# Sample attention's tables made in the projections and kept in memory, x2's first part normalised beside sample attention, and gating sums taken three chunks at a time

## The chip, the cores and the metric

The kernel runs on one core of one Trainium2 chip, as one program. The metric is the device time of one execution in microseconds (us). A core has TensorE (PE; its weight loads are listed as PEld), VectorE (DVE), ScalarE (ACT), GpSimd (POOL), SyncE (SP, which only issues transfers) and 16 DMA engines. Each engine takes its instructions in the order in which they stand.

## The reference, cut to what matters

One layer of a hybrid decoder for a prompt (1024 rows) and a sample group (8 sequences of 8 new rows, 2048 past rows in a paged cache), 1088 rows in all, width 1024, everything in float32:

```python
x = x + 0.5 * swiglu(rmsnorm(x)) @ wd            # FFN1, width 2816
u = rmsnorm(x) @ w_in                            # q, k/v of three branches, gates, z, xBC, dt
y = rmsnorm_groups(ssd(silu(conv(xBC))) * silu(z)) * ssm_norm      # Mamba-2, 8 heads, chunks of 128
o = g0 * compressed(q) + g1 * selected(q) + g2 * window(q)         # attention, with ALiBi slopes
x = x + concat(o, y) @ w_out
x = x + 0.5 * swiglu(rmsnorm(x)) @ wd2           # FFN2
out = rmsnorm(x)
```

For the sample rows attention needs constant tables: ALiBi biases by position (for compressed, selected, window and new rows), masks, a triangle for ranking the blocks, and one-hot matrices that spread gates and sum groups of rows. They depend on no input but their shape.

## The kernel before, in words

Activations lie transposed: features on the 128 partitions, rows along the free dimension, 1088 of them in two halves `b` of 544, each half in two parts (`SUBS`: 256 and 288 columns). x lies in `xT`, eight tiles of 128 features. Part z=0 is the first 256 columns of each half, z=1 the other 288. Products in float32 are made of three products of a high part (`whi`, `hh`, `oh`) and a low part (`wlo`, `hl`, `ol`), in `mm3` (L237); ScalarE casts the high part and VectorE or POOL subtracts for the low one (L229, L258). The FFNs go through 2x2 blocks with seven products (`B1`..`B7`, `dq`).

A scheduler places the instructions: the code's order is the starting point, and the order on each engine comes from a planner with its own costs. The kernel's stages, in time:

1. FFN1, then its down projection (`D1.products`, L590): products into `dq` on TensorE, eight banks; VectorE adds each to xT (L618).
2. The norm of x: for each feature tile ScalarE squares and POOL or VectorE adds into `rms` (`row_sq`, L768), the scaled x is split into `hh` and `hl` (`row_split`, L778). `rms_row` (L803) sums over the partitions with five small products against `ones` (bank `nps`), takes the root and the reciprocal, and spreads the factor over the partitions by products with `ident` (`nR`). The half b=1 comes first, then b=0.
3. Projections: eight xBC groups (L238; `xbc_chunk` evacuates a bank into `xr`, which takes the factor `rms`), convolution, then z, then the Mamba scan (`scan`, L1069). `mamba_setup` makes `BD`, six 32x512 blocks of decay sums in bfloat16 (`blocks_of`, L1051), which the first products `ar` (L1105) of chunks 0 to 7 read.
4. Keys and values (`proj`, `keys`, `cmp_products`), and between them `gate` (L1196) for each of nine chunks: z from memory into `za`, times y, square on ScalarE, one addition (L1203), two sums over the partitions by products against `ones` (bank `yn`, L1206), a copy into `yr`. After chunks 6 and 8 the root and reciprocal, and products `yR` that spread the factor.
5. q, then the prompt's attention in eight tiles of 128 queries (`KN["qt"]`), with the sample's compressed rows between. The last tile ends it. VectorE takes the maximum of each score bank, ScalarE the exponential (L1660), POOL or VectorE scales, TensorE transposes (`pT`) and multiplies by the values (`o`).
6. Sample attention (`sample_attention`, L1716): first its tables (`bsel`, `bwin`, `bnew`, `bcmp`, `tri`, `G`, `E`, `hsel`, `idx4`, `oneh`), then, for four pairs of sequences, rows gathered by POOL's indirect transfers (`schk`), and scores. Between them stand the output projection's products (`wout`): y for z=0, attention's rows for z=0, y for z=1. With each z=0 tile of x2 that is done, ScalarE squares and VectorE adds into `acc20` (`x2_sq`, L2075).
7. The rest of the output projection (attention's rows for z=1), beside which z=0's norm is finished (`x2_rms(0)`), its eight rows of h are made in `hp` (`h_row`, L2149) and split into B1..B7 (`b0`, L2160), and z=1's squares are added into `acc` (L2084). `x2_rms(1)` follows, and FFN2 begins with `g` (L398).
8. FFN2 and the last norm.

Pools hand memory on: a tile of a new pool waits for the last use of what lay there before.

Of the kernel before, what the change touches and what calls it, by code (L numbers as in the profile page):

```python
# [17 lines left out]
P = 128  # L18
# [62 lines left out]
def hybrid_step(ctx: ExitStack, tc: tile.TileContext, *aps):  # L81
# [16 lines left out]
    zD = DR.tile([4, P, T], F32, name="zD")  # L98

# [703 lines left out]
    def rms_row(v, n):  # L803

        q = side("nps")
        parts = blocks(n)
        for i, m in parts:
            nc.tensor.matmul(q[:m, i:i + 1], v[:, P * i:P * i + m], ones[:, :1], start=True, stop=True,
                             skip_group_check=True)
# [27 lines left out]
    WA = Ahead(Ws.enter_context(pool("w", bufs=8, side="right")))  # L837
# [25 lines left out]
    with pool("cv", bufs=2) as K:  # L863
# [39 lines left out]
        stT = K.tile([P, 8, 24], F32, name="stT", bufs=1)  # L903
        for group in [(0, 1)] + [(i,) for i in range(2, 8)]:
# [9 lines left out]
            for i in group:  # L914
                xbc_end(i, *ws[i][1:])
        for z in range(2):
# [33 lines left out]
    def mamba_setup(K, K2, Q, acs_bank):  # L950
# [100 lines left out]
        def blocks_of(z):  # L1051
# [12 lines left out]
        for z in range(2):  # L1064
            blocks_of(z)
# [130 lines left out]
    def gate(K, yr, c):  # L1196
# [6 lines left out]
        nc.vector.tensor_tensor(za[:, ::2, :L], za[:, ::2, :L], za[:, 1::2, :L], op=OP.add)  # L1203
        q = side("yn")
        for g in range(2):
            nc.tensor.matmul(q[:L, g:g + 1], za[:, 2 * g, :L], ones[:, :1], start=True, stop=True,  # L1206
                             skip_group_check=True)
        nc.vector.tensor_copy(yr[:L, c], q[:L, :2])
        if c in (6, 8):
            v = yr[:, :7] if c == 6 else yr[:, 7:]  # L1210
            nc.vector.tensor_scalar(v, v, 1.0 / 256, EPS, op0=OP.mult, op1=OP.add)
            nc.scalar.activation(v, v, AF.Sqrt)
            nc.vector.reciprocal(v, v)
            t0, n = SUBS[c // 8]
            for t0 in (t0, HALF + t0):
# [58 lines left out]
    with pool("kvtmp", bufs=2) as K:  # L1274
# [118 lines left out]
        for c in range(2):  # L1393
            gate(K, yr, c)
# [5 lines left out]
        for c in range(2, 4):  # L1400
            gate(K, yr, c)
# [6 lines left out]
        for c in range(4, 7):  # L1408
            gate(K, yr, c)
        cmp_finish(1, ab)  # L1410
        v2 = proj(2, 1)
        keys(2, k2)
        natural(2, (k2, v2))
        for c in range(7, 9):
            gate(K, yr, c)
    Ds = ExitStack()
# [913 lines left out]
```

## Time and profile before

| | |
|---|---|
| median of 3 runs | 2544.39 us (2540.56 to 2546.0) |
| the profiled execution's own time | 2548.51 us |
| its span in the profile | 2546.8 us, mean granted clock 0.971 |
| TensorE busy | 2439.3 us (96%) |
| VectorE busy | 1759.6 us (69%) |
| ScalarE busy | 1116.8 us (44%) |
| POOL busy | 430.4 us (17%) |
| moved by DMA | 371.90 MB, 146 GB/s |

Times in the rows are counted from the start of the span. A row of a timeline is a group of equal neighbours: start, time from the first's start to the last's end, engine, line, operation, result from operands, count; in brackets the idle time before it and what released it. Neighbours on one engine overlap by some hundredths of a microsecond. [...]

### The profile page before, as it was taken

Reading aid. Unit: us, or ns where it says so; the run is one execution under the profiler, and the core shown is the slowest. Engines: PE = TensorE matmul, PEld = TensorE weight load, DVE = VectorE, ACT = ScalarE, POOL = GpSimd, SP = SyncE. Lnnn points to the kernel's source line nnn. Section 1 sums busy time; section 2 is a strip of 40 time slices with the busy share of each in tenths; the row PEclk is TensorE's granted clock in tenths of the full one; section 3 lists DMA queues with packets and bytes.
Section 4 is the critical chain, followed back from the end, with each engine's and each line's share of the span. In section 5 each row is a group of like instructions: output and inputs, shape, how many; then the busy total and the mean of one; then the engine's idle time right before and its main releaser. Section 6 shows DMA issues by size and latency. Waiting matters only on the chain.

```text
span 2546.8 us, 48004 instructions
## 1 busy us (share of the span) xinstructions
PE 2439.3 (96%) x18979; PEld 2241.6 (88%) x18979; DVE 1759.6 (69%) x3676; ACT 1116.8 (44%) x2461; POOL 430.4 (17%) x530
## 2 busy tenths in 40 slices
PE   6999999999999989899999998998799999999998
PEld 6999999999999978898677766566799999999998
DVE  6767677677777655666566677666877776768776
ACT  7544444441242253225566675443544444443113
POOL 0000000011133343434333342221100000001110
PEclk9999999999999999999999999899899999999999
DMA  4334343597652323323010110666233444459754
GB/s 164 123 125 160 126 159 133 176 354 283 223 185 80 104 72 113 94 79 116 34 67 34 42 59 1 222 201 210 79 112 131 156 146 153 149 190 372 254 207 150
DMA packets 226269, 371.90 MB, mean 146 GB/s; under 512 B 18173, under 2 KB 143785, under 8 KB 224892
## 3 DMA queue, kind: packets, MB, share of 16 engines
q1 hardware_dynamic: 207112, 311.92, 35.8%
q0 software_dynamic: 7600, 38.59, 4.3%
q10 hardware_dynamic: 11332, 18.33, 1.9%
q8 instruction: 149, 2.44, 0.4%
q14 instruction: 76, 0.62, 0.1%
HBM read 250.84 MB, written 122.07 MB: 146 GB/s over the span
## 4 chain that ended last, share of the span: by engine, by line
PE 83%; DVE 8%; ACT 3%; DMA 3%; issue 1%; POOL 0%; ACTq 0%; DVEq 0%; SPq 0%; POOLq 0%
PE gY L353 6%; PE gY L354 6%; PE gY L352 6%; PE dq L609 5%; PE dq L610 5%; PE dq L611 5%; PE gX L353 4%; PE gX L354 4%; PE gX L352 4%; PE o L1691 3%; PE pT L1682 3%; PE s L1644 1%; PE cA L1569 1%; PE xbc L238 1%; PE cA L1571 1%
## 5 line engine op out<-in xcount | busy, mean ns | idle before, releaser
L610 PE MATMUL dq<-db,da 128*128 128x256 f32 (+1 forms) x1232 | 352.8, 287 | 0.3 <-DVE da L258 0.3
L611 PE MATMUL dq<-db,da 128*128 128x256 f32 (+1 forms) x1232 | 352.4, 287 | 0.0
L609 PE MATMUL dq<-db,da 128*128 128x256 f32 (+1 forms) x1232 | 349.0, 288 | 2.9 <-DVE xT L255 1.5
L618 DVE TENSOR_TENSOR xT<-xT,dq 128x256 f32<-128x256 f32 (+1 forms) x456 | 186.6, 434 | 82.7 <-PE dq L611 81.0
L609 PEld LDWEIGHTS dq<-db,da 128*128 128x128 f32 x1232 | 229.8, 188 | 4.2 <-DVE xT L255 1.7
L258 POOL TENSOR_TENSOR ds<-dw 128x512 f32<-128x512 f32 x22 | 28.6, 1299 | 1208.2 <-DMA dw<-in_ffn_wd_dram 988.4
L611 PEld LDWEIGHTS dq<-db,da 128*128 128x128 f32 x1232 | 232.3, 189 | 0.0
L610 PEld LDWEIGHTS dq<-db,da 128*128 128x128 f32 x1232 | 231.2, 188 | 0.6 <-DVE da L258 0.5
L255 ACT CAST whi<-ws 128x512 fp32r<-128x512 f32 x156 | 96.4, 622 | 210.5 <-PE gY L354 144.7
L258 DVE TENSOR_TENSOR wlo<-raw,whi 128x512 fp32r<-128x512 f32 x180 | 123.0, 688 | 79.2 <-ACT whi L255 78.9
L255 ACT CAST da<-ds 128x512 fp32r<-128x512 f32 x88 | 52.8, 626 | 236.9 <-PE dq L611 92.5
L255 ACT CAST whi<-raw 128x512 fp32r<-128x512 f32 x184 | 113.9, 625 | 65.9 <-PE gY L354 20.0
L1660 ACT ACTIVATE pb<-s,mx 128x256 f32<-128x256 f32 (+3 forms) x192 | 105.1, 552 | 74.3 <-DVE mx L1658 38.8
L258 DVE TENSOR_TENSOR wlo<-ws,whi 128x512 fp32r<-128x512 f32 x156 | 106.8, 688 | 42.2 <-ACT whi L255 41.7
L1682 PEld LDWEIGHTS pT<-ident,pb 128*128 128x128 f32 x528 | 60.8, 147 | 49.7 <-issue 40.9
L1657 DVE TENSOR_REDUCE mx<-s 128x1 f32<-128x384 f32 (+2 forms) x128 | 66.6, 536 | 40.8 <-PE s L1649 27.5
L1682 PE MATMUL pT<-ident,pb 128*128 128x128 f32 x528 | 90.8, 290 | 3.5 <-ACT pt L255 1.5
L352 PE MATMUL gY<-B3h,whi 128*128 128x256 f32 (+1 forms) x320 | 91.5, 287 | 1.4 <-ACT whi L255 1.4
L353 PE MATMUL gX<-B6h,wlo 128*128 128x256 f32 (+1 forms) x320 | 91.8, 287 | 0.5 <-DVE wlo L258 0.5
L352 PE MATMUL gX<-B6h,whi 128*128 128x256 f32 (+1 forms) x320 | 91.4, 286 | 0.9 <-ACT Cc L359 0.9
L353 PE MATMUL gY<-B3h,wlo 128*128 128x256 f32 (+1 forms) x320 | 91.7, 287 | 0.2 <-DVE wlo L258 0.2
L353 PE MATMUL gY<-B2h,wlo 128*128 128x256 f32 (+1 forms) x320 | 91.8, 287 | 0.0
(714 smaller groups left out, 8603.5 us busy)
## 6 DMA issues: line engine op xcount, KB each, us to landing
db<-GD SPq DMA_DIRECT2D x42, 1632.0 KB
GD<-Cc SPq DMA_DIRECT2D x154, 272.0 KB
GD<-his SPq DMA_DIRECT2D x84, 272.0 KB
raw<-in_ffn_wg_dram SPq DMA_DIRECT2D x22, 1024.0 KB
raw<-in_ffn_wu_dram SPq DMA_DIRECT2D x22, 1024.0 KB
dw<-in_ffn_wd_dram SPq DMA_DIRECT2D x44, 512.0 KB
GD<-hp SPq DMA_DIRECT2D x70, 272.0 KB
db<-GD SPq DMA_DIRECT2D x14, 1088.0 KB
```

The costliest lines, as they stand in the source:

```text
L255: return nc.scalar.copy(out, src) if eng == "a" else ENGINES[eng].tensor_copy(out, src)
L258: ENGINES[eng].tensor_tensor(out, x, y, op=op)
L352: nc.tensor.matmul(q, ah[:, k], b_, start=first, stop=False, skip_group_check=True)
L353: nc.tensor.matmul(q, al[:, k], b_, start=False, stop=False, skip_group_check=True)
L354: nc.tensor.matmul(q, ah[:, k], c_, start=False, stop=(k == 3), skip_group_check=True)
L609: nc.tensor.matmul(q, x, bh[:, u, o], start=first, stop=False, skip_group_check=True)
L610: nc.tensor.matmul(q, y, bh[:, u, o], start=False, stop=False, skip_group_check=True)
L611: nc.tensor.matmul(q, x, bl[:, u, o], start=False, stop=(u == np_ - 1), skip_group_check=True)
L618: nc.vector.tensor_tensor(x, x, q, op=OP.subtract if i == 4 else OP.add)
L1660: nc.scalar.activation(pb[:, st:st + pn], s, AF.Exp, bias=mx[:, 0:1], accum_out=part[:, hh_, i:i + 1])
L1682: nc.tensor.transpose(tq_[:kn, P * hh_:P * hh_ + P], src, ident)
L1691: mm = nc.tensor.matmul(O[64 * u:64 * u + 64], v_, p_, start=(ui < 2), skip_group_check=True, stop=(ui - len(held) + 1 + u >= len(units) - 2))
```

## The change

Four parts.

- **Tables.** `sample_constants` holds what stood at the head of `sample_attention`. It is called within the xBC groups, after group 3; all but `idx4` and `oneh` go into slices of one tile `big` (128 x 4552 float32), which is written to memory (`saD`). In sample attention `big` is read back. The pool of weight tiles `w` has 7 buffers in place of 8.
- **Decay blocks.** The six multiplications of `BD` are POOL's, and the `bd_b` tile has three buffers.
- **Gating.** `gate` leaves the added squares of a chunk in `hs`; `gate_sums` makes the products for three chunks in one bank, with one copy; `gate_norm` takes the root and spreads the factors once, at the end.
- **The second norm.** z=0's norm stands right after z=0's last tile of x2, and its rows of h overwrite x2's z=0 tile (which is first stored to `xD`). For z=1 TensorE sums the squares: five products per tile add up in one bank (`sums`), and VectorE's additions into `acc` are gone. The pools `x20`, `ha` and `wa` are opened in another order, and `acc20` lies in `ha`.

```diff
@@ projections
-    WA = Ahead(Ws.enter_context(pool("w", bufs=8, side="right")))
+    WA = Ahead(Ws.enter_context(pool("w", bufs=7, side="right")))
...
+        def sample_constants(SC, Q):
+            big = Q.tile([P, 4552], F32, name="big")
...
+            nc.vector.tensor_tensor(bsel, bc[:, None, :].to_broadcast([P, 16, P]),
+                                    bs[:, :, None].to_broadcast([P, 16, P]), op=OP.add)
...
+            nc.sync.dma_start(saD, big)
+            return idx4, oneh
...
+            if group[0] == 3:
+                with pool("sac0") as Q:
+                    sa_const = sample_constants(M, Q)
@@ mamba_setup
-                b = Q.tile([96, P], BF16, name="bd_b", bufs=1)
+                b = Q.tile([96, P], BF16, name="bd_b", bufs=3)
...
-                nc.vector.tensor_tensor(D[d], b[d, None, :].to_broadcast([32, 4, P]),
+                nc.gpsimd.tensor_tensor(D[d], b[d, None, :].to_broadcast([32, 4, P]),
                                         hm[d, :, None].to_broadcast([32, 4, P]), op=OP.mult)
@@ gating
-    def gate(K, yr, c):
+    def gate(K, hs, c):
...
-        nc.vector.tensor_tensor(za[:, ::2, :L], za[:, ::2, :L], za[:, 1::2, :L], op=OP.add)
+        nc.vector.tensor_tensor(hs[:, :, :L], za[:, ::2, :L], za[:, 1::2, :L], op=OP.add)
+
+    def gate_sums(yr, hs, cs):
         q = side("yn")
-        for g in range(2):
-            nc.tensor.matmul(q[:L, g:g + 1], za[:, 2 * g, :L], ones[:, :1], start=True, stop=True,
-                             skip_group_check=True)
-        nc.vector.tensor_copy(yr[:L, c], q[:L, :2])
+        for j, c in enumerate(cs):
+            L = P if c < 8 else TS
+            for g in range(2):
+                nc.tensor.matmul(q[:L, 2 * j + g:2 * j + g + 1], hs[:, j, g, :L], ones[:, :1], start=True, stop=True,
+                                 skip_group_check=True)
...
@@ sample_attention
-        pi = SC.tile([P, 1], I32, name="pi")
-        nc.gpsimd.iota(pi, pattern=[[0, 1]], base=0, channel_multiplier=1)
...
+        big = SC.tile([P, 4552], F32, name="big")
+        nc.sync.dma_start(big, saD)
+        bsel = big[:, :2048].rearrange("p (s c) -> p s c", s=16)
...
+        idx4, oneh = sa_const
@@ output projection and second norm
+    x2_rms(0)
+    for m in range(KD):
+        h_row(m, 0, X2[0][:, m])
     hy = out_h(HA, yT, 1)
...
     def b0(kk):
-        x, y = (h_row(m, 0, FX.tile("hp", [P, 576], 5)) for m in (kk, kk + 4))
-        b_make(0, kk, h_of(x, y))
+        b_make(0, kk, h_of(X2[0][:, kk], X2[0][:, kk + 4]))
+    sums = side("nps")
     ws = [out_w(WA, 0, m, "vp"[m % 2]) for m in range(KD)]
     for m in range(KD):
         out(ws[m], ha, m, 1)
         if m in B0AT:
             b0(B0AT.index(m))
-        x2_sq(m, 1)
-    x2_rms(1)
+        sq = FX.tile("hp", [P, 576], 5)
+        nc.scalar.activation(two(sq), xz(m, 1), AF.Square)
+        for i, n in blocks(576):
+
+            nc.tensor.matmul(sums[:n, i:i + 1], sq[:, P * i:P * i + n], ones[:, :1], start=(m == 0 and i == 0),
+                             stop=(m == KD - 1), skip_group_check=True)
+    acc2[1] = FX.tile("acc", [P, 576])
+    x2_rms(1, sums)
```

The order moves with it. VectorE at the end of the down projection, before (xT with dq: the additions of products to x; hl: low parts for the first norm's half; da: a factor of the last products):

```order
961 L258 TENSOR_TENSOR da_8843<-ds_8852,da_8843 128x512
962 L783 SCALAR_TENSOR_TENSOR hl_6234<-xT_6344,vec,hh_6233 128x544
963 L618 TENSOR_TENSOR xT_6343<-xT_6343,dq 128x256
964 L618 TENSOR_TENSOR xT_6343<-xT_6343,dq 128x288
965 L618 TENSOR_TENSOR xT_6343<-xT_6343,dq 128x256
966 L618 TENSOR_TENSOR xT_6343<-xT_6343,dq 128x288
967 L618 TENSOR_TENSOR xT_6343<-xT_6343,dq 128x256
968 L618 TENSOR_TENSOR xT_6343<-xT_6343,dq 128x288
969 L618 TENSOR_TENSOR xT_6343<-xT_6343,dq 128x256
970 L618 TENSOR_TENSOR xT_6343<-xT_6343,dq 128x288
971 L618 TENSOR_TENSOR xT_6344<-xT_6344,dq 128x256
972 L783 SCALAR_TENSOR_TENSOR hl_6234<-xT_6343,vec,hh_6233 128x544 x2
```

and now (L959, L963, L955, L972: bcmp, bwin, bsel and d of the tables; L619 is the addition, one line further down):

```order
976 L954 TENSOR_SCALAR bs<-bs,slope 128x16
977 L959 TENSOR_SCALAR big<-big,mt,slope 128x127
978 L619 TENSOR_TENSOR xT_6344<-xT_6344,dq 128x256
979 L1050 TENSOR_SCALAR An<-An 128x8
980 L963 TENSOR_SCALAR big<-iw,cols 128x512
981 L619 TENSOR_TENSOR xT_6344<-xT_6344,dq 128x288
982 L955 TENSOR_TENSOR big<-bc,bs 128x2048
983 L619 TENSOR_TENSOR xT_6344<-xT_6344,dq 128x256
984 L972 TENSOR_SCALAR d_9795<-d_9795,b_9797 128x256
985 L619 TENSOR_TENSOR xT_6344<-xT_6344,dq 128x288
986 L619 TENSOR_TENSOR xT_6344<-xT_6344,dq 128x256
987 L619 TENSOR_TENSOR xT_6344<-xT_6344,dq 128x288
```

The additions, which stood in a row, have table work between them; the other tables stand in the rows around.

POOL around the first decay blocks, now (before, no BD row stands on POOL, and ea follows st):

```order
102 L230 TENSOR_TENSOR wlo<-raw,whi 128x512 x2
103 L259 TENSOR_TENSOR st<-st,cdec 128x512
104 L1155 TENSOR_TENSOR BD_10592<-bd_b,hm 32x512 x3
105 L1155 TENSOR_TENSOR BD_10605<-bd_b,hm 32x512 x3
106 L259 TENSOR_TENSOR ea<-ea,xbc 128x512 x2
107 L259 TENSOR_TENSOR st<-st,cdec 128x512
```

All six blocks stand between the first state product st and the first products ea.

TensorE at the end of the output projection, before (wout: the product of attention's rows; nps and nR: the norm's sums and its factor):

```order
11262 L238 MATMUL wout<-oh,whi 128x288
11263 L239 MATMUL wout<-oh,wlo 128x288
11264 L240 MATMUL wout<-ol,whi 128x288
11265 L238 MATMUL wout<-oh,whi 128x288
11266 L239 MATMUL wout<-oh,wlo 128x288
11267 L240 MATMUL wout<-ol,whi 128x288
11268 L808 MATMUL nps<-ones,acc 128x1 x4
11269 L808 MATMUL nps<-ones,acc 64x1
11270 L217 MATMUL nR<-ident,nr 128x128 x4
11271 L818 MATMUL nps<-ident,nr 128x64
11272 L398 MATMUL g_21381<-B1h_20834,whi 128x256
```

and now, in the midst of the same products:

```order
11244 L241 MATMUL wout<-ol,whi 128x288
11245 L2207 MATMUL nps<-ones,hp 128x1 x4
11246 L2207 MATMUL nps<-ones,hp 64x1
11247 L239 MATMUL wout<-oh,whi 128x288
11248 L240 MATMUL wout<-oh,wlo 128x288
11249 L241 MATMUL wout<-ol,whi 128x288
11250 L239 MATMUL wout<-oh,whi 128x288
11251 L240 MATMUL wout<-oh,wlo 128x288
11252 L241 MATMUL wout<-ol,whi 128x288
11253 L239 MATMUL wout<-oh,whi 128x288
11254 L240 MATMUL wout<-oh,wlo 128x288
```

The sums, which stood once behind the last product, now stand in eight places between the products (L2207).

## Rows read from the trace of the kernel before

**Rows 1.** the page's first part: busy time and its share of the span by engine
```profile
PE 2439.3 (96%) x18979; PEld 2241.6 (88%) x18979; DVE 1759.6 (69%) x3676; ACT 1116.8 (44%) x2461; POOL 430.4 (17%) x530
```
**Rows 2.** waits of TensorE by cause, 700 to 1900: us in total, times, longest
```profile
PE nps L808 <- DVE acc L2084: 11.4, 1, 11.4
PE s L1644 <- ACT pb L1660: 9.4, 15, 1.8
PE yn L1206 <- DVE za L1203: 5.3, 1, 5.3
...
PE ar L1105 <- DVE BD L1061: 4.7, 1, 4.7
PE nR L217 <- DVE nr L215: 4.4, 2, 3.5
...
PE xs_ps L1083 <- DVE st L1148: 1.7, 1, 1.7
```
**Rows 3.** windows: length, busy per engine (instructions), granted clock, DMA share, GB/s
```profile
1570.00:1575.00 5.00, 5.00 (x42) 3.88 (x42) 4.73 (x28) 2.40 (x8) 4.93 (x12) 1.00 0.00 0
1575.00:1590.00 15.00, 8.38 (x40) 5.58 (x36) 14.68 (x54) 5.97 (x23) 1.59 (x3) 0.70 0.00 1
1605.00:1610.00 5.00, 4.04 (x19) 2.99 (x19) 3.99 (x10) 3.98 (x9) 0.00 (x0) 0.50 1.04 394
```
**Rows 4.** VectorE's timeline 1571 to 1594: start, us, line, operation [idle before]
```profile
1573.00 0.07 DVE L1739 MEMSET slv<- 128x1 f32 x2
...
1579.13 0.35 DVE L1786 TENSOR_SCALAR d<-d,b 128x256 f32<-128x256 f32 x1
...
1585.56 2.29 DVE L1768 TENSOR_TENSOR bsel<-bc,bs 128x2048 f32<-128x2048 f32 x1
...
1588.56 1.14 DVE L1790 TENSOR_SCALAR d<-d,cols,slope 128x256 f32<-128x256 f32 x1
...
1590.69 0.39 DVE L1791 TENSOR_TENSOR bnew<-d,v 128x256 f32<-128x256 f32 x1
```
**Rows 5.** windows at the end of the down projection and the second norm
```profile
755.00:770.00 15.00, 12.70 (x90) 12.43 (x90) 15.00 (x19) 11.30 (x19) 8.78 (x6) 0.89 0.52 164
770.00:775.00 5.00, 4.17 (x32) 3.78 (x31) 3.99 (x6) 2.53 (x5) 1.33 (x2) 1.00 0.55 155
775.00:780.00 5.00, 4.02 (x20) 3.63 (x20) 1.65 (x8) 0.95 (x3) 0.10 (x1) 0.55 0.00 0
```
**Rows 6.** VectorE's timeline, 744 to 784
```profile
754.84 0.45 DVE L618 TENSOR_TENSOR xT<-xT,dq 128x288 f32<-128x288 f32 x1 [0.77 <-PE dq L611]
...
770.12 4.19 DVE L776 TENSOR_TENSOR rms<-rms,nsq 128x544 f32<-128x544 f32 x4
...
779.27 0.72 DVE L879 TENSOR_TENSOR xr<-xbc,rms 128x256 f32<-128x256 f32 x2 [2.44 <-PE nps L818]
```
**Rows 7.** POOL's timeline, 1571 to 1600
```profile
1588.36 1.19 POOL L258 TENSOR_TENSOR pc<-pc,sm 128x512 f32<-128x512 f32 x1 [6.12 <-DVE sm L1667]
```
**Rows 8.** VectorE's timeline, 893 to 906
```profile
896.26 0.67 DVE L1061 TENSOR_TENSOR BD<-bd_b,hm 32x512 bf16<-32x512 bf16 x1
...
898.50 0.68 DVE L1061 TENSOR_TENSOR BD<-bd_b,hm 32x512 bf16<-32x512 bf16 x1
```
**Rows 9.** window of the gating wait
```profile
1070.00:1075.00 5.00, 0.88 (x5) 0.91 (x5) 4.87 (x9) 4.34 (x8) 1.34 (x1) 0.74 0.33 95
```
**Rows 10.** VectorE's timeline, 1779 to 1832
```profile
1811.93 0.74 DVE L2149 SCALAR_TENSOR_TENSOR hp<-xT,vec,acc 128x512 f32<-128x512 f32 x1
1812.59 0.75 DVE L2084 TENSOR_TENSOR acc<-acc,xs 128x576 f32<-128x576 f32 x1
```
**Rows 11.** TensorE's timeline, 1778 to 1836
```profile
1821.49 2.17 PE L808 MATMUL nps<-ones,acc 128*128 128x1 f32 x10 [11.40 <-DVE acc L2084]
1827.12 2.08 PE L217 MATMUL nR<-ident,nr 128*128 128x128 f32 x8 [3.46 <-DVE nr L215]
```
**Rows 12.** ScalarE's timeline, 1778 to 1830
```profile
1782.25 1.28 ACT L214 ACT_TABLE_LOAD   x1
```

More of the change, by code (lines that the diff above doesn't have):

```diff
@@ L98, in hybrid_step @@
     zD = DR.tile([4, P, T], F32, name="zD")
+    saD = DR.tile([P, 4552], F32, name="saD")
     xs2 = A["x_sample"].rearrange("b t d -> (b t) d")
@@ L801, in row_done, with rms_row @@
             late_rows.append(m)
-    def rms_row(v, n):
-        q = side("nps")
+    def rms_row(v, n, q=None):
         parts = blocks(n)
-        for i, m in parts:
-            nc.tensor.matmul(q[:m, i:i + 1], v[:, P * i:P * i + m], ones[:, :1], start=True, stop=True,
-                             skip_group_check=True)
+        if q is None:
+            q = side("nps")
+            for i, m in parts:
+                nc.tensor.matmul(q[:m, i:i + 1], v[:, P * i:P * i + m], ones[:, :1], start=True, stop=True,
+                                 skip_group_check=True)
         r = NP.tile([P, len(parts)], F32, name="nr")
@@ L1049, in mamba_setup @@
         BD = []
-        def blocks_of(z):
+        for z in range(2):
             D = K.tile([96, 4, P], BF16, name=f"BD{z}", bufs=1)
@@ L1392, in hybrid_step @@
         natural(0, (k0, v0))
-        for c in range(2):
-            gate(K, yr, c)
+        hs = K.tile([P, 3, 2, P], F32, name="hs", bufs=1)
+        for c in range(3):
+            gate(K, hs[:, c], c)
         k1 = proj(1, 0)
@@ L1399, in hybrid_step @@
         positions(0)
-        for c in range(2, 4):
-            gate(K, yr, c)
+        gate_sums(yr, hs, range(3))
+        hs = K.tile([P, 3, 2, P], F32, name="hs", bufs=1)
+        for c in range(3, 5):
+            gate(K, hs[:, c - 3], c)
         cmp_finish(0, ab)
@@ L1407, in hybrid_step @@
         positions(1)
-        for c in range(4, 7):
-            gate(K, yr, c)
+        gate(K, hs[:, 2], 5)
+        gate_sums(yr, hs, range(3, 6))
+        hs = K.tile([P, 3, 2, P], F32, name="hs", bufs=1)
+        gate(K, hs[:, 0], 6)
         cmp_finish(1, ab)
@@ L1412, in hybrid_step @@
         keys(2, k2)
+        for c in range(7, 9):
+            gate(K, hs[:, c - 6], c)
         natural(2, (k2, v2))
-        for c in range(7, 9):
-            gate(K, yr, c)
+        gate_sums(yr, hs, range(6, 9))
+        gate_norm(yr)
     Ds = ExitStack()
@@ L1792, in sample_attention @@
-        tri = SC.tile([P, 31, 31], F32, name="tri")
-        nc.gpsimd.memset(tri, 1.0)
-        nc.gpsimd.affine_select(out=tri, in_=tri, pattern=[[1, 31], [-1, 31]], compare_op=OP.is_gt, fill=0.0,
-                                base=0, channel_multiplier=0)
+        big = SC.tile([P, 4552], F32, name="big")
+        nc.sync.dma_start(big, saD)
+        bsel = big[:, :2048].rearrange("p (s c) -> p s c", s=16)
+        bwin = big[:, 2048:2560].rearrange("p (s c) -> p s c", s=4)
+        bnew = big[:, 2560:2816].rearrange("p (s c) -> p s c", s=4)
@@ L2103, in hybrid_step, with side, x2_rms, h_row @@
         out(ws[i], ha, m, 0)
-        x2_sq(m, 0)
+        x2_sq(m)
+    wn2 = col["norm_ffn2"]
+    NP = WA
+    def side(name):
+        return PO.tile([P, 512], F32, name=name, tag="wout")
+    def x2_rms(z, q=None):
+        rms_row(acc2[z], 2 * SUBS[z][1], q)
+        c0, n = SUBS[z]
+        for b in range(2):
+            for m in range(0, KD, 4):
+                (nc.sync if z else nc.scalar).dma_start(xD[:, m:m + 4, HALF * b + c0:HALF * b + c0 + n],
+                                                        X2[z][:, m:m + 4, n * b:n * b + n])
+    def h_row(m, z, tile):
+        h = tile[:, :2 * SUBS[z][1]]
+        nc.vector.scalar_tensor_tensor(two(h), xz(m, z), wn2[:, m:m + 1],
+                                       two(acc2[z]), op0=OP.mult, op1=OP.mult)
+        return h
+    x2_rms(0)
+    for m in range(KD):
+        h_row(m, 0, X2[0][:, m])
     hy = out_h(HA, yT, 1)
```

214 lines of the change are left out of this document (102 added, 112 removed).

## The prediction

> **What bounds the kernel now.** [...] The list of TensorE's waits by cause then names the idle stretches [rows 2]: 11.4 us for the sums of the second norm's z=1 rows (acc), 9.4 us in 15 pieces for attention's exponentials, 5.3 us for a gating sum (za), 4.7 us for a decay block (BD), 4.4 us in two pieces for a norm's nr. The change touches nearly all of these places. Then I read each place in windows and on VectorE's timeline.
>
> **Tables out of attention's end.** In 1570 to 1575 TensorE works without a gap at a granted clock of 1.00; in the next 15 us it works 8.38 of them while VectorE works 14.68; and in 1605 to 1610 the clock is 0.50, half speed [rows 3]. VectorE's work there is partly the tables: 40 small instructions from the first slv at 1573.00 to bnew at 1590.69, 11.5 us by their durations and some 9.5 us net of the overlap of neighbours, bsel alone 2.29 [rows 4]. The exponentials wait behind them (VectorE makes their maxima), which is the 9.4 us of [rows 2]. All 40 go. VectorE keeps about 8 us of attention's own work in these 18, and the chain score, maximum, exponential, transpose remains. Lower bound of the gain: 5 us, half the net table time, if the chain of the softmax sets the end. Upper bound: 15, the idle 6.6 us of 1575 to 1590 and 8 us of clock, half of the time from 1590 to 1605 or so. I take 11, the net 9.5 and a little of the clock, since TensorE ran dense at 1.00 just before.
>
> What comes in their place is one load of big, 2.33 MB. By the built program it waits for attention's last compress product on TensorE and not for attention's end, and the DMA engines stand idle from 1570 to 1590 (share 0.00 in both windows of [rows 3]). At the 394 GB/s of 1605 to 1610 it takes 5.9 us, which that gap holds, ahead of the first reader, whose place comes after attention's last product. Cost 0; if that cover were gone, up to 6. The gathers of sample rows are queued on POOL behind attention's last products and move up with them; the DMA share of 1.04 [rows 3] says that the sample stage will take part of the gain back, which my 11 against 15 allows for.
>
> **Tables into the projections.** The diff puts them after the fourth xBC group, but the built order has them much earlier: on VectorE they stand among the last additions into xT of the down projection, ahead of the first norm's rows. There VectorE has no room: in 755 to 770 it is busy 15 of 15 us, and in 770 to 775 3.99 of 5 [rows 5]. The additions end at 755.3, the second norm's sums (rms) at 774.3, and the first xr that frees banks in number comes at 779.27 [rows 6]; TensorE, which has 8 banks, fills them meanwhile and runs out: 4.17 and 4.02 of 5 us in 770 to 780, at 0.55 [rows 5]. Nearly every xr stands behind the second norm on VectorE, so what is put ahead of that norm delays all of them. Net table work 9.5 us, less the 0.8 us for which VectorE waited for a product at 754.84 [rows 6]: 9 us, all of it on the path, since nothing later makes it up where TensorE is the bound. Lower bound 3: matrix columns already waiting let TensorE work through the wait, and VectorE has gaps after 775 (1.65 of 5 [rows 5]) into which some of the order's tail (bnew, idx4) may fall. Upper bound 13, from contention: a 128x256 TENSOR_SCALAR takes 0.35 us, and 1.14 while POOL's pc runs for 1.19 [rows 4, 7], 0.66 us lost per us of POOL; the tables bring with them most of the 4.93 us that POOL works in 1570 to 1575 [rows 3] and a little from before, so 4 more.
> [...]
> The store of the tables (saD, 2.33 MB, on SP) stands ahead of later w_in loads and waits for bnew; by [rows 5] the DMA share there is 0.55 and below, and the loads run some groups ahead, so 0, with 3 us as the bound. One weight buffer less (8 to 7): 0, bound 2.
>
> **Decay blocks on POOL.** Six multiplications of 0.67 us leave VectorE [rows 8]. On POOL I price each at 1.19, the pc row [rows 7]; three stand before the first ar product. Now the first begins at 896.26 and the third ends at 899.18 [rows 8]; on POOL three take 3.6 us, from the same start to 899.9. So the 4.7 us stay, plus 0.7; the next wait, 1.7 us for the state addition behind the second half's blocks [rows 2], goes. Sum: 1 us gained. Bounds: 3 gained if VectorE's price holds on POOL, 3 lost if a product takes POOL 2 us (it holds the ea products behind).
>
> **Gating by three chunks.** The sum of the third chunk stands on TensorE where its operand is late: 5.3 us of wait, 1070 to 1075 is busy for 0.88 us and 0.74 granted [rows 2, 9]. After the change the sum of three chunks stands some 5 us of kv products later and its operand earlier on VectorE, ahead of the KA splits. Gain 5.3 less about 0.8 for what KA itself makes late; the same four loops of yR follow, bunched. I take 4.5; bounds 6.5 gained (with the clock), 2 lost (the yR group at the end waits for one chain of copy, root and reciprocal).
>
> **The second norm.** VectorE sets the pace of this stage: its rows stand without idle time ahead [rows 10], and TensorE waits 11.4 us for the last of them. Eight rows of h (0.74, 0.66 from start to start) and seven additions to acc (0.75, about as much net) leave it: 10 us [rows 10]. The sums for z=1 are then 8 groups of ten small products on TensorE; ten take 2.17 us at half clock [rows 11], 1.09 at full, so 40 blocks less the 5 of before cost 7.6 us. z=0's eight products leave the stage's start, 1.7 by the same row. TensorE's other products ended at 1810.1 and it stood until 1821.49; now they end at 1810.1 + 7.6 - 1.7 = 1816. The last ten then take 1.1, and the chain from there to nR takes the 3.5 us that it took, 1823.7 to 1827.12 [rows 11]: nR at 1820.6, 6.5 us sooner, and 1 more since TensorE is idle for a shorter time and the clock falls less: 7.5 gained. Against it, the z=0 norm and its eight rows (5.4 us) run beside sample attention, on the same VectorE, and two more table loads of 1.28 come in [rows 12]; the rows overwrite x2 and so wait for its store. Cost 1.5, bounds 0 and 6. Net 6; bounds 11 gained, 1 lost.
> [...]
>
> **Sum**: -11 + 9 - 1 - 4.5 - 6 = -13.5 us on the profiled execution's own 2548.5, so 2535. Its time is 4.1 above the median of the three runs (2544.4), to which I carry the difference: **2531**.
>
> **Rivals.**
> *The tail pays more than the rest earns.* One mechanism: at the end of the down projection VectorE is already the later engine, so tables and contention cost 13, and xT additions behind them hold product banks, a further 3; the other gains come in at their poorer half (5, 0, 3, 2: 10). 10 - 16 = +6: 2550. It decides when TensorE's gap before xr passes 13 us. For it: 15 of 15 busy [rows 5]. Against: gaps after 775. Chance 0.17.
> *Sample attention gives the gain back.* Its gathers come at a share of 1.04 of the DMA engines [rows 3]; attention ends earlier, and TensorE waits for sample rows, and for the stores of x2 besides. Attention's gain shrinks to 5, the second norm's to 4: -5 + 9 - 1 - 4.5 - 4 = -5.5 at most, with 2 us more of waits -3.5: 2541. Chance 0.18.
> *The tail has room.* If the tables fall into waits there (cost 3) and attention's end comes back at full clock (15): -15 + 3 - 1 - 5.5 - 7.5 = -26: 2518. Chance 0.15.
> *The tables stay where they are in time* (the order is what was built, not the diff's place): excluded by the order.
>
> **Chances.** The forecast has 0.50 and holds 2525 to 2537. The range, 2517 to 2550, takes in the larger part of both outer rivals. About 0.2% (5 us) can be told from no change here: faster 0.66 (forecast, room in the tail and a little of the second rival), same 0.16, slower 0.18.
>
> **What would show it.** Right: in 1575 to 1605 VectorE well under 80% and a clock of 1.00, attention over some 11 us sooner; the second norm of the projections some 9 us later after the last dq product, with TensorE idle or at half clock there; no wait at yn; the wait for BD unchanged in size; the wait before the last nps under 3 us. Wrong: if xr is not late (then faster than I say), if first sample products wait for big, or if the waits for gathered rows pass 10 us in all.

## The result, and the profile after

The changed kernel takes **2519.39 us** (median of 4 runs, 2517.19 to 2521.26), the kernel before 2545.19 beside it: a ratio of 0.9901, 95% interval 0.9883 to 0.9918. Timed again on another chip (run e12) it took 2520.66 against 2543.79: 0.9912, 0.9894 to 0.9930. So 23 to 26 us are gone, where 13.5 were forecast. The execution profiled after took 2521.26 us, with a span of 2519.6 and a mean granted clock (TensorE's, as a share of full speed) of 0.979 (0.971 before).

The page's first part after, to set against [rows 1]: TensorE lost 7.5 us of busy time and gained 70 instructions.

```profile
PE 2431.8 (97%) x19049; PEld 2240.9 (89%) x19049; DVE 1750.6 (69%) x3656; ACT 1118.0 (44%) x2462; POOL 432.1 (17%) x537
```

TensorE's waits by cause, whole run (us in total, times, longest), to set against [rows 2]. The 11.4 for acc and the 5.3 for za are gone, the exponentials' 9.4 is 3.5, the decay block's 4.7 is 5.0, and new are the 4.5 for whi and the 2.3 for xT, both at the end of the down projection.

```profile
PE ar L1197 <- POOL BD L1155: 5.0, 1, 5.0
PE kT_ps L1941 <- DMA schk<-in_cache_sel_dram,idx: 4.6, 3, 2.2
PE xbc L239 <- DVE whi L229: 4.5, 1, 4.5
PE s L1750 <- ACT pb L1766: 3.5, 9, 0.7
PE dq L610 <- DVE xT L619: 2.9, 2, 2.3
```

Where the time went is read from marks, the first or last start of one tile's products in each profile. Two of them, as the view of a tile on TensorE prints them (count: duration min/median/max in ns, first to last start in us): the first norm's sums (`nps`, each half ten of the 20) and attention's values (`o`).

```profile
L810 PE MATMUL nps<-ones,rms x20: 166/250/271, 763.5 to 787.5; 128*128 128x1 f32 x16, 128*32 128x1 f32 x4
L1797 PE MATMUL o<-pt,VAc x32: 589/614/641, 1199.6 to 1578.2; 64*64 64x512 f32 x32
```

Before, the same lines end at 775.4 and 1603.8. The table has, for every kernel of this study, the last nps of the first norm and then lengths between marks: last nps to first ar, first ar to last kv, last q to last o (attention), last o to last a_ps (sample attention), last a_ps to the last small product that spreads the second norm's factor (nps from nr). Each row is read from one profile, and the execution profiled lies up to 5.2 us from the median in the column of times, so a difference of 2 or 3 us between two rows may be chance.

| kernel | last nps | to ar | ar to kv | attention | sample | second norm | time | ratio, 95% |
|---|---|---|---|---|---|---|---|---|
| before | 775.4 | 123.9 | 214.6 | 431.7 | 175.1 | 50.5 | 2544.39 | |
| after | 787.5 | 123.3 | 206.2 | 404.2 | 178.1 | 45.9 | 2519.39 | 0.9883-0.9918 |
| e12 after again | 784.6 | 123.3 | 208.9 | 404.2 | 179.2 | 45.2 | 2520.66 | 0.9894-0.9930 |
| e1 gating alone | 775.0 | 121.4 | 204.9 | 419.1 | 176.2 | 50.9 | 2522.35 | 0.9893-0.9932 |
| e2 tables alone | 783.9 | 122.9 | 214.3 | 421.5 | 172.5 | 50.5 | 2539.35 | 0.9968-0.9990 |
| e3 without gating | 784.4 | 123.2 | 210.9 | 417.7 | 176.8 | 45.1 | 2536.57 | 0.9960-0.9987 |
| e4 without tables | 775.9 | 121.8 | 207.9 | 418.9 | 181.7 | 46.7 | 2528.01 | 0.9917-0.9956 |
| e5 tables at k, v | 773.8 | 124.5 | 223.7 | 404.2 | 178.4 | 45.9 | 2528.18 | 0.9920-0.9962 |
| e6 tables in scan | 775.8 | 123.9 | 221.3 | 417.1 | 176.8 | 46.6 | 2536.32 | 0.9955-0.9980 |
| e7 tables in scan | 771.1 | 123.2 | 224.4 | 408.6 | 184.8 | 44.7 | 2530.42 | 0.9919-0.9958 |
| e8 without norm | 786.1 | 123.3 | 208.4 | 405.2 | 176.1 | 50.1 | 2523.97 | 0.9897-0.9946 |
| e9 tables held | 772.9 | 127.7 | 204.3 | 404.2 | 180.0 | 45.1 | 2514.04 | 0.9866-0.9908 |
| e10 held, two parts | 772.3 | 127.0 | 207.8 | 408.4 | 173.6 | 51.3 | 2514.11 | 0.9856-0.9904 |
| e11 held in portions | 774.4 | 121.8 | 207.6 | 405.9 | 178.0 | 45.9 | 2512.41 | 0.9862-0.9901 |

From before to e12 the marks say: 9.2 us later at the last nps, then 0.6, 5.7, 27.5 sooner in three stretches (and 1.1 between kv and q), 4.1 later in sample attention and 5.3 sooner at the second norm. The last nps has a part of chance: in the first 100 us, unchanged code, half clock cost 10.2 us before and in e12, 13.7 in the first profile of after and 6.8 in e9 (5-us windows, one minus the granted clock, times 5, summed).

**The tail of the down projection.** Windows after (length, busy per engine, granted clock, DMA share, GB/s), to set against [rows 5]: VectorE is full for 35 us, and TensorE has all but stopped at 765.

```profile
740.00:755.00 15.00, 12.67 (x91) 12.11 (x90) 14.97 (x40) 6.51 (x11) 10.61 (x18) 0.91 0.20 76
755.00:765.00 10.00, 8.16 (x63) 7.83 (x62) 10.00 (x18) 8.44 (x14) 9.08 (x7) 0.96 0.29 113
765.00:770.00 5.00, 0.76 (x3) 0.80 (x4) 5.00 (x15) 4.09 (x7) 1.34 (x1) 0.60 0.05 20
770.00:775.00 5.00, 4.16 (x19) 3.81 (x18) 5.00 (x11) 0.00 (x0) 0.00 (x0) 0.50 0.97 307
```

VectorE's timeline there, to set against [rows 6]: table rows stand between additions into xT, and the last addition, 754.84 before, starts at 768.31. The 128x8 comparison takes 3.07 us, to which I come back at the end.

```profile
746.29 3.07 DVE L924 TENSOR_SCALAR big<-big,cols 128x8 f32<-128x8 f32 x1
...
751.68 2.29 DVE L955 TENSOR_TENSOR big<-bc,bs 128x2048 f32<-128x2048 f32 x1
...
760.43 1.85 DVE L965 SCALAR_TENSOR_TENSOR big<-iw,slope,big 128x512 f32<-128x512 f32 x1
...
768.31 0.44 DVE L619 TENSOR_TENSOR xT<-xT,dq 128x288 f32<-128x288 f32 x1
...
790.42 0.72 DVE L881 TENSOR_TENSOR xr<-xbc,rms 128x256 f32<-128x256 f32 x2 [1.50 <-PE nps L820]
```

**Attention's end.** Windows after, to set against [rows 3]: full clock to 1580, and in the last of them VectorE is busy for 10.35 of 15 us, where it was 14.68; the load of big runs beside it at a DMA share of 0.43 and 0.47.

```profile
1550.00:1565.00 15.00, 14.79 (x106) 10.38 (x105) 13.30 (x48) 9.82 (x32) 3.67 (x7) 1.00 0.43 155
1565.00:1580.00 15.00, 12.43 (x73) 7.04 (x71) 10.35 (x42) 9.56 (x35) 6.90 (x8) 1.00 0.47 151
```

**Attention's middle**, which I had not looked at. Two windows of it before, then the same two after: 0.93 and 0.95 of full clock have become 1.00 and 0.98.

```profile
1150.00:1250.00 100.00, 95.02 (x617) 73.58 (x616) 57.86 (x141) 53.02 (x134) 37.45 (x69) 0.93 0.27 95
1350.00:1450.00 100.00, 95.66 (x627) 70.98 (x625) 60.63 (x140) 58.68 (x157) 31.87 (x46) 0.95 0.11 43
```
```profile
1150.00:1250.00 100.00, 95.30 (x656) 73.86 (x655) 58.47 (x126) 58.65 (x144) 35.62 (x57) 1.00 0.29 100
1350.00:1450.00 100.00, 97.43 (x673) 73.66 (x671) 63.73 (x155) 65.19 (x177) 37.82 (x55) 0.98 0.13 46
```

**Decay blocks and the second norm.** POOL's and TensorE's timelines after, to set against [rows 8] and [rows 11]: a block takes 1.03 to 1.07 us on POOL, ar waits 5.01; the last sums of the second norm wait 1.32 us, and nR follows 0.98 after them.

```profile
907.18 1.03 POOL L1155 TENSOR_TENSOR BD<-bd_b,hm 32x512 bf16<-32x512 bf16 x1 [0.90 <-DVE bd_b L1151]
908.43 1.07 POOL L1155 TENSOR_TENSOR BD<-bd_b,hm 32x512 bf16<-32x512 bf16 x1 [0.23 <-DVE bd_b L1151]
```
```profile
910.76 1.01 PE L1197 MATMUL ar<-BD,sel 96*128 96x512 bf16 x2 [5.01 <-POOL BD L1155]
...
1796.74 2.15 PE L2207 MATMUL nps<-ones,hp 128*128 128x1 f32 x10 [1.32 <-ACT hp L2204]
1799.88 2.08 PE L218 MATMUL nR<-ident,nr 128*128 128x128 f32 x8 [0.98 <-DVE nr L216]
```

### The profile page after: what moved, and what is told of

The parts are those of the page before. It is cut to its first block, busy times and chain, and to the rows that moved or that the text cites. A ratio compares the mean times of both kernels' runs of the same rounds, so it can differ in the third digit from the quotient of the medians.

```text
span 2519.6 us, 48128 instructions
## 1 busy us (share of the span) xinstructions
PE 2431.8 (97%) x19049; PEld 2240.9 (89%) x19049; DVE 1750.6 (69%) x3656; ACT 1118.0 (44%) x2462; POOL 432.1 (17%) x537
## 4 chain that ended last, share of the span: by engine, by line
PE 87%; DVE 6%; DMA 3%; ACT 2%; issue 1%; SPq 0%; POOL 0%; ACTq 0%; DVEq 0%
PE gY L354 6%; PE gY L355 6%; PE gY L353 6%; PE dq L610 6%; PE dq L611 6%; PE dq L612 6%; PE gX L354 5%; PE gX L355 5%; PE gX L353 5%; PE o L1797 3%; PE pT L1788 3%; PE s L1750 1%; PE xbc L240 1%; PE xbc L239 1%; PE xbc L241 1%; PE cA L1675 1%
## 5 line engine op out<-in xcount | busy, mean ns | idle before, releaser
L619 DVE TENSOR_TENSOR xT<-xT,dq 128x256 f32<-128x256 f32 (+1 forms) x456 | 186.9, 433 | 83.9 <-PE dq L612 82.4
L266 POOL TENSOR_TENSOR pb<-pb,sm 128x640 f32<-128x640 f32 (+7 forms) x70 | 85.0, 1236 | 40.0 <-DVE sm L1773 34.1
```

The lines of the kernel that those rows point to most:

```text
L266: nc.gpsimd.tensor_tensor(out, x, by.to_broadcast(list(x.shape)), op=OP.mult)
L619: nc.vector.tensor_tensor(x, x, q, op=OP.subtract if i == 4 else OP.add)
```

## The experiments

**First question: whose are the 27.5 us of attention?** The sum had 11 for the tables at its end. But the scheduler laid out all of attention anew: of the 2644 rows that TensorE has from the first score to the last o, a longest-match comparison pairs only 46% in the orders before and after, though the change has no line there. In the order before, the first compress product (cA) comes 13.2 us after the last q product, in the one after 17.9. Programs with one part alone, built and not all of them run, tell which part draws which order: the second norm and the decay blocks alone leave the order before, row for row; seven weight buffers alone give a third order (64% like before, 52% like after), which e2 and e3 have but for the tables' neighbours; with gating by three chunks besides it is the order after (99% in e1, 98% in e4, whose differences are the tables' neighbours at the end). The shares in the expectations below are of the first three quarters of these rows; those of the whole are 92% of before and 43% of after for e6, 72% and 32% of after and before for e7.

e1, gating alone:

```diff
 before.py
-    WA = Ahead(Ws.enter_context(pool("w", bufs=8, side="right")))
+    WA = Ahead(Ws.enter_context(pool("w", bufs=7, side="right")))
-            gate(K, yr, c)
+            gate(K, hs[:, c], c)
...
+        gate_sums(yr, hs, range(3))
```


> Gating by three chunks alone (with the weight pool at 7 buffers, which its tiles need); tables, decay blocks and second norm as before. Three theories. Sum of the parts: gating gives 5 us and nothing else changes, 2540. Redrawn order: the planner lays out the whole of attention anew as soon as gating changes (the order of attention's products on TensorE here is word for word that of the changed kernel, 46% like the one before), and that order is what made attention's middle 10 us shorter: 2530, with some 2 us lost to half clock between the start of attention and its last tile (1.7 in the changed kernel) where the kernel before loses 12. Chance of the clock: the 10 us belong to no part; half-clock spells in that stretch appear in some programs or executions and not in others, 2540 with anything from 2 to 12 us lost.

Measured: 2522.35, ratio 0.9912 (0.9893 to 0.9932), as much as the whole change and 8 us below the lowest of the three times expected. First ar to last kv is 9.7 us shorter and attention 12.6, with the tables still at its end; 5.1 us of half clock between 1150 and 1550, 12.0 before.

e2, the tables alone:

```diff
 before.py
+    saD = DR.tile([P, 4552], F32, name="saD")
+                    sa_const = sample_constants(M, Q)
+        nc.sync.dma_start(big, saD)
```


> The tables alone are made early and pass through memory (weight pool at 7 buffers); the rest as before. Sum of the parts: the first norm of the projections 8 us later, attention's end 11 to 15 us shorter, so 2538 to 2542. Redrawn order: attention has a third order here (69% like the one before on TensorE, 53% like the changed kernel's), so its middle may be anything between the two, 2528 to 2542; the sample stage gives back up to 3. If instead the tables made the middle faster, 2528.

Measured: 2539.35, 0.9979 (0.9968 to 0.9990). The last nps is 8.5 us later, attention 10.2 shorter, sample attention 2.6 shorter.

e3, the changed kernel with gating as before:

```diff
 after.py
-            gate(K, hs[:, c], c)
+            gate(K, yr, c)
```


> The changed kernel with gating as before: a sum for every chunk. Sum of the parts: the 5 us of gating are lost, 2524. Redrawn order: attention's order is that of the kernel with the tables alone, so its middle is as there; if it loses the 10 us that attention's middle gained, 2534. The wait for the third chunk's sum returns at some 5 us in either case.

Measured: 2536.57, 0.9973 (0.9960 to 0.9987): 16 to 17 us slower than the changed kernel. First ar to last kv gives 4.7 or 2.0 of it (after, e12), attention 13.5, with tables, norm and decay blocks as in the changed kernel.

e4, the changed kernel with the tables where they were:

```diff
 after.py
-                    sa_const = sample_constants(M, Q)
-        big = SC.tile([P, 4552], F32, name="big")
+        bsel = SC.tile([P, 16, P], F32, name="bsel")
```


> The changed kernel with the tables back at the head of sample attention. Sum of the parts: 8 us gained at the first norm, 15 lost at attention's end, 2526. Redrawn order: attention's order on TensorE is word for word that of the changed kernel, so its middle keeps the 10 us: 2526 as well, with some 2 us of half clock between the start of attention and its last tile. If the tables were what shortened the middle, 2536 and some 12 us of half clock there.

Measured: 2528.01, 0.9936 (0.9917 to 0.9956). The last nps returns to 775.9, attention is 14.7 us longer, sample attention 2.5 to 3.6. Its windows at attention's end: VectorE is busy for 14.17 of the 15 us from 1550, and TensorE's clock is 0.54 there.

```profile
1540.00:1550.00 10.00, 9.24 (x67) 6.78 (x65) 9.08 (x41) 6.79 (x21) 7.94 (x17) 1.00 0.00 0
1550.00:1565.00 15.00, 11.59 (x39) 6.44 (x39) 14.17 (x44) 3.37 (x11) 1.14 (x3) 0.54 0.00 0
1565.00:1580.00 15.00, 13.41 (x66) 10.30 (x66) 10.54 (x45) 8.42 (x32) 6.79 (x8) 0.66 0.31 106
```

So the two are separate: 14.7 us for the tables at an equal order, some 12.7 for the order with the tables in place (431.7 against 419.1 and 418.9). What remained was whether gating shortens attention by itself, and not by the order.

**Second question: is it the order, and do the tables cost time wherever they are made?** The next three move the call of `sample_constants`; all four parts are in.

```diff
 after.py, e5
-            if group[0] == 3:
...
+    SSs.close()
+    with pool("sac0") as Q:
+        sa_const = sample_constants(M, Q)
 after.py, e6 (e7: behind scan)
+    with pool("sac0") as Q:
+        sa_const = sample_constants(M, Q)
     scan(SSM, *ssc)
```


> The changed kernel with the tables made at the head of keys and values in place of the end of the down projection (call moved behind the z products). Attention's order on TensorE is word for word that of the changed kernel. Theory (tables cost 8 to 9 where VectorE is the later engine, nothing where TensorE is): the second nps group back some 9 us sooner, attention from the last q product to the last o product 404 us as in the changed kernel, and 2511, with up to 4 given back in the keys and values, where VectorE is busy 6.4 to 9.8 of 10 us: 2515. Rival (the tail's 9 us were half clock and chance, not the tables): 2519. Rival (keys and values wait for the tables' memory): 2522.

> The changed kernel with the tables made in the scan (call just before it; two scratch tiles lie inside big). All four parts of the change are in, but attention's order on TensorE is 91% that of the kernel before and 42% that of the changed kernel. Redrawn order: attention from the last q product to the last o product takes 417 us (before's 432 less the 15 of the tables) and not 404, so the 9 us gained at the down projection are lost again: 2524. Gating itself shortens attention, by whatever way: 404 us and 2511.

> As the run before, with the call just behind the scan in the code; VectorE's order has the tables in the scan all the same. Attention's order on TensorE is 64% that of the changed kernel and 27% that of before. Redrawn order: attention takes something between 404 and 417 us, so 2511 to 2524, and differs from the run before by more than 3 us although both make the tables in the scan. Order without effect: the same time as the run before within 3 us.

Measured: e5 2528.18 (0.9941), e6 2536.32 (0.9968), e7 2530.42 (0.9938). All three came out slower than the times expected for them. On the length of attention the expectation held to a tenth: attention took 417.1 in e6, which has gating by three chunks, early tables and an order 92% that of before, and 404.2 in e5 with the order of after. e7's fourth order gives 408.6. Over all kernels without tables in attention, the order of after gave 404.2 to 408.4 in seven profiles; e2, e3 and e6, each in another order, gave 417.1 to 421.5. So the redrawn order is shown for these three; e7's 408.6 can't be told from the seven.

The granted clock shows how the order costs time. All of attention in one window, in e6 and in e5:

```profile
1178.00:1595.00 417.00, 405.06 (x2658) 290.76 (x2657) 269.70 (x644) 267.09 (x716) 159.09 (x236) 0.96 0.15 56
```
```profile
1179.00:1583.00 404.00, 390.73 (x2658) 282.18 (x2657) 265.16 (x644) 265.57 (x716) 155.74 (x233) 1.00 0.15 55
```

TensorE stands idle for 11.9 us in the one and 13.3 in the other, so idle time is not the difference. One minus the granted clock, times the length from the last q to the last o, is 15.4 us in e6 and 0 in e5; it is 16.4 in e2, 11.3 in e3, 0 to 6.8 in the seven profiles with the order of after, and 23.4 before. (It is somewhat more than what the clock cost, since idle time at half clock counts too.) In e3, 7.9 of the 11.3 lie behind 1550, at attention's end, which no table reaches there.

On the tables I was wrong: the tail's time came back (last nps at 771 to 776), but first ar to last kv grew from 206.2 (208.9 in e12) to 221.3, 223.7 and 224.4, more than the tail had cost. TensorE's waits in e6 in the scan, and in e5 in keys and values (us in total, times, longest):

```profile
PE y L1218 <- DVE de L259: 12.3, 3, 7.9
```
```profile
PE nat_ps L1406 <- DVE KAc L1467: 7.3, 1, 7.3
...
PE pcA L239 <- ACT KA L1439: 4.9, 1, 4.9
```

VectorE's mean share is about half in the scan (38.96 of 80 us in 920 to 1000 after), and I had read room from that. The scheduler put the tables at the scan's head, between `de` rows for which y waits, and beside POOL's rows. Whether e5's waits come from the tables' rows or from memory that the tables held was not taken apart.

e8, the changed kernel with the second norm as before:

```diff
 after.py
-    x2_rms(0)
-    for m in range(KD):
-        h_row(m, 0, X2[0][:, m])
...
-        sq = FX.tile("hp", [P, 576], 5)
-        nc.scalar.activation(two(sq), xz(m, 1), AF.Square)
+        x2_sq(m, 1)
```


> The changed kernel with the second norm as before. Attention's order on TensorE is that of the changed kernel. From the stages of the runs so far: from the last a_ps to the last nR 5 us longer, from the last o to the last a_ps 4 to 5 us shorter: 2519 to 2520. By the prediction's step (6 us net): 2525. If the rows of h beside sample attention cost more than z=1's sums bring: 2515.

Measured: 2523.97, 0.9922 (0.9897 to 0.9946); the interval does not tell it from the changed kernel. By marks the norm's stage is 4.2 to 4.9 us longer and sample attention 2.0 to 3.1 shorter.

**Third question: is there a place where the tables are free?** In 820 to 870, among the xBC groups, TensorE had no gap, and each bank that VectorE empties is one of the four that the xBC products take in turn. There the code has the tables, but the scheduler had drawn them ahead. e9 queues them on VectorE and on POOL behind the last instruction of the fourth group; e10 does so with gating and tables alone; e11 hands them out in four portions.

```diff
 after.py, e9
-                with pool("sac0") as Q:
+                with pool("sac0") as Q, tc.issue_after(conv.ins), tc.issue_after(keep.ins):
                     sa_const = sample_constants(M, Q)
 after.py, e11
+            if 2 <= i <= 2+3:
...
+                with tc.issue_after(conv.ins), tc.issue_after(keep.ins):
+                    made = next(making)
```


> The changed kernel with the tables held where its code has them: on VectorE and on POOL they are queued behind the last instruction of the fourth xBC group, where the planner had drawn them ahead of the first norm. Attention's order on TensorE is word for word that of the changed kernel. In 820 to 870 TensorE has no gap and full clock, VectorE is busy 38 of 50 us, and a late bank can wait for VectorE since there are eight. Theory (tables cost time only where a chain stands behind VectorE, as at the norm, at the scan's head and at the head of keys and values): second nps group 8 to 12 us sooner than in the changed kernel, nothing lost in the xBC groups, attention 404 us: 2509 to 2512. Rival (VectorE has no room here either, since 38 of 50 with 10 more and contention is full): ar late again by 5 to 9 us, 2516 to 2520. Rival (tables made anywhere cost 15, as in the three runs that moved them): 2526.

> As the run before, but with the decay blocks on VectorE and the second norm as in the kernel before: gating and tables alone. Attention's order on TensorE is that of the changed kernel. By the stages so far the second norm is worth 0 to 2 us net and the decay blocks 1 to 3: 2 to 4 us slower than the run before, 2512 to 2515. By the prediction's terms (6 and 1): 7 us slower. If rows of h beside sample attention cost what z=1's sums bring: no difference.

Measured: e9 2514.04 (0.9887, 0.9866 to 0.9908), e10 2514.11 (0.9880, 0.9856 to 0.9904). The last nps comes at 772.9 and attention keeps 404.2, but last nps to first ar is 127.7. So e9's time lies above 2509 to 2512. The norm and the decay blocks together are worth nothing that can be measured here (0.1 us between medians of four runs each; by their profiles e9 is 5.7 us faster, since its profiled execution was the fastest of four and e10's the second slowest). In other company they are worth something, and not always the same: with the tables in sample attention they cost 5.7 us (2528.01 in e4 against 2522.35 in e1, on one chip, with no run of the one within the other's), with the tables moved and gating as before they gain 2.8 (e3 against e2, on that chip too).

> The changed kernel with the tables held in the xBC groups as in the run e9, but in four portions, behind the third, fourth, fifth and sixth group. In e9, ar begins 10 us sooner than in the changed kernel where the last nps group is 14.6 us sooner: 4.5 are lost in the xBC groups, 2.3 of them a wait for xr at the place where the tables stand in one bunch, and half-clock time behind it. Theory (the bunch costs that, since VectorE falls behind by more than the eight banks hold): from the last nps group to the first ar product 123 to 125 us instead of 127.7, and the time 3 to 4 us under e9's by its stages, 2510. Rival (the tables and POOL's part of them slow VectorE wherever they are): the same 127.7 and no difference.

> The changed kernel itself, beside the run above on the same chip, to compare with it directly and to see how far a second profile's half-clock time differs. Its ratio to the kernel before should be 0.988 to 0.992. Half-clock time in the first 100 us, where nothing is changed, was 13.7 us in its first profile and 7 to 10 in others: if that is chance it falls elsewhere this time. In attention, 2 us or less lost between its start and its last tile, and 404 us from the last q product to the last o product.

Measured beside each other on one chip: e11 2512.41 (5 runs, 2509.68 to 2515.59), e12 2520.66 (6 runs, 2518.53 to 2523.81). e11 is 8.2 us faster, and no run of the one reaches into those of the other. Last nps to first ar is 121.8 where e9 had 127.7, so by the marks what the bunch cost is gone; by their ratios to the kernel before, 0.9882 and 0.9887, e11 and e9 can't be told apart. TensorE has no gap in 820 to 870 with VectorE busy for 48.90 of 50 us:

```profile
820.00:870.00 50.00, 50.00 (x400) 49.90 (x400) 48.90 (x78) 9.11 (x12) 18.65 (x28) 1.00 0.43 139
```

The same window of e9, with the tables in one bunch:

```profile
820.00:870.00 50.00, 47.51 (x367) 47.08 (x366) 46.73 (x87) 9.22 (x12) 22.26 (x26) 0.97 0.40 133
```

e11 beats both kernels of this case. By its direct comparison with e12 it leads by 8.2 us, near the 10 us by which its last nps comes sooner (774.4 against 784.6, with equal half clock in the first 100 us).

## Why the prediction was right, and why its size was not

Sign and range held (2531 forecast, 2517 to 2550; 2519 measured). The sum was 13.5 us and the gain 23 to 26. Step by step:

- **Missing from the sum: the order of attention, some 12.7 us.** The step that failed is the silent one that work which the diff doesn't touch stays as it is. I had compared the built order at the tail and not in attention, where it would have shown 46%. One weight buffer less, put at 0, redraws attention by itself, and gating besides it gives the order of after. What that order changed is time at half clock: 15.4 us of attention in e6, 0 in e5. In e3 it is not all: taken off, e3's attention is still 4 us longer than that of after (11.3 off 417.7, 1.7 off 404.2). Which rows of the order make the clock fall was not taken apart.
- **Tables out of attention's end, -11 forecast (5 to 15): -14.7** (e4 to after, 418.9 to 404.2), near the upper bound. That bound counted the idle time and the half clock, and both went. I took less because sample attention would take part back; without the tables at its head it became 2.5 to 3.6 shorter instead (e4 to after and e12). No wait of TensorE names the load of big. One reading was wrong: of the 9.4 us of waits for the exponentials only 5.4 lie behind the first row of the tables at 1573.00, the others between 1178 and 1556; at attention's end 0.9 are left of the 5.4.
- **Tables into the tail, +9 (3 to 13): about +10**, right (last nps of e12 against e11, 10.2; e2 against before, 8.5). The mechanism was the one given: xr starts at 790.42 for 779.27, and TensorE stops behind 96 xBC products in both profiles, which fill four banks of 24 products each and not the eight that I counted. Contention is in it, as the 128x8 row shows: 3.07 us beside POOL's rows, 0.22 in e11, where POOL stood idle. The bound of 13 priced contention from one pair of rows (0.66 us lost per us of POOL); the runs, 10.2 and 8.5, lie nearer the net 9.
- **Decay blocks, -1 (-3 to +3): not told from 0.** The wait is 5.0 for 4.7, as forecast. First ar to last kv, with and without the part, differs by -3.4 (e3 against e2), -3.5 (e9 against e10) and +3.0 (e4 against e1), and by 2.7 between after and e12, the same kernel.
- **Gating, -4.5 (-6.5 to +2): about -6.** First ar to last kv is 213.3 in the mean of the three kernels with a sum for every chunk, 207.0 in that of the eight with three chunks whose tables are not made in that stretch. The wait for za is gone and none came in its place.
- **The second norm, -6 net: about 0 beside the tables in the projections.** Its own stage gave what was worked out, 6.2 us from e10 to e9 against 7.5. The mis-sized term is the cost beside sample attention, taken as 1.5 with bounds 0 and 6: sample attention is 6.4 longer from e10 to e9, 5.5 from e1 to e4, 2.0 to 3.1 from e8 to after and e12. With the tables in sample attention it does not earn its price at all (e1 to e4, with the decay blocks: 5.7 us slower). "On the same VectorE" should have been priced at the rows' whole 5.4 us in a stage whose chains already run through VectorE.

With the measured sizes, the decay blocks and the norm at 0: -14.7 - 12.7 + 10 - 6 + 0 = -23.4. The forecast's error is mostly two terms of opposite sign, the order (-12.7) and the norm (+6), and 3.7 of the tables.

Of the rivals, the time fell on that of the third, 2518, but not by its way: the tail had no room (VectorE 5.00 of 5 in 765 to 775). The first, a tail that costs 16, did not happen. Of the second, sample attention grew by 3 to 4 us, not by waits for gathered rows (4.6 in all, below the 10 named) but by the norm's rows. Most of the signs named came out: no wait at yn, 1.32 before the last nps, 5.0 for BD, the first norm's second half 9 to 12 late. Two did not. The stretch from 1575 to 1605 can't be read for attention's end, since attention had ended at 1578. And attention, said to be over some 11 us sooner, took 27.5 us less: that sign pointed at the missing term.

## What to carry to other kernels

Where a scheduler sets the order, compare the built orders over the whole program before pricing a change: an edit may redraw a stage that it doesn't touch, and that redraw can be as large as everything the edit was made for (12.7 of 25 us here), with a sign that no row of the trace before told. Work off the critical engine is not free because that engine's mean share is low: the same tables cost 10 us at a norm, 12 to 18 at the head of the scan or of keys and values, and nothing that shows in portions beside products that take four banks in turn; ask which chain stands behind each row. And if the code names a place for such work, see whether the built order kept it there.

## What the runs showed of the hardware that I had not expected

A short row of VectorE can last through several rows of POOL. The 128x8 comparison of the tables took 0.22 us in e11, where POOL stood idle; 3.07 and 3.06 in the two profiles of the changed kernel; 5.84 in e9. POOL's timeline of e9 at that row:

```profile
817.77 0.91 POOL L980 MEMSET big<- 128x961 f32 x1
818.62 0.19 POOL L988 MEMSET oneh<- 32x128 bf16 x1
...
818.83 2.53 POOL L230 TENSOR_TENSOR wlo<-raw,whi 128x512 fp32r<-128x512 f32 x2
821.33 1.28 POOL L981 TENSOR_SCALAR_AFFINE_SELECT big<-big 128x961 f32<-128x961 f32 x1
822.57 0.28 POOL L989 TENSOR_SCALAR_AFFINE_SELECT oneh<-oneh 32x128 bf16<-32x128 bf16 x1
822.82 0.94 POOL L1019 MEMSET raw<- 128x1024 f32 x1
823.72 0.28 POOL L991 TENSOR_SCALAR_AFFINE_SELECT oneh<-oneh 32x128 bf16<-32x128 bf16 x1
```

VectorE's row in the same stretch starts at 817.95 and ends at 823.79, as the POOL row of 822.82 does (823.76), though one more POOL row follows that without a gap:

```profile
817.95 5.84 DVE L925 TENSOR_SCALAR big<-big,cols 128x8 f32<-128x8 f32 x1
```

In the changed kernel it starts at 746.29 and ends at 749.36, again with the end of a POOL row (748.44 + 0.89 = 749.33). In e6 the 64x512 comparison took 3.50 us from 909.94 beside three POOL products that end at 913.15, and 0.47 in e9, where it starts at 824.09 and POOL's last row had ended at 824.00. The 128x8 row did not end with the POOL instruction that ran as it began: counted from that one, its end came with the eighth in e9 and with the fourth in the changed kernel, and POOL had no gap between them. What ties the two engines there, no run shows. The one row of e9 lasted 5.6 us longer than in e11, and last nps to first ar 5.9; whether the portions as such or this row alone made that difference was not tested.
